# First products with both parts of x as one moving operand of 512 columns, from the fortieth tile on

## The chip, the cores and the metric

The kernel runs on one core of one Trainium2 chip. The core has a matmul engine (TensorE; its weight loads are listed apart as PEld), a vector engine (DVE), a scalar engine (ACT), a general engine (POOL) and a queue engine (SP) that starts transfers. Each takes its own instructions in the order in which the program lists them, and they wait for each other by semaphores. The metric is the time of one execution on the device in microseconds; the number for a kernel is the median of its runs. Before the change it is 1940.97 us, three runs from 1940.72 to 1942.93.

## The reference

Two layers of a decoder trunk on 256 tokens of width 1024. The part that the change touches is the second half of a layer, a retrieval over 16384 experts:

```python
q = (xf @ wq).reshape(T, PEER_HEADS, 2, PEER_KEY_DIM)
s = jnp.einsum('thcd,ckd->thck', q, subkeys).astype(jnp.float32)
sv, si = lax.top_k(s, PEER_TOPK)
...
experts = (ea * PEER_KEYS + eb).reshape(T, PEER_HEADS * PEER_TOPK)
gate = jax.nn.softmax(cv, axis=-1).reshape(T, PEER_HEADS * PEER_TOPK)
...
act = jax.nn.gelu(jnp.einsum('cd,ced->ce', xc, u_tab[ec]))
return jnp.einsum('ce,ced->cd', act * gc, v_tab[ec])
```

Each token takes 128 of the 16384 experts, multiplies itself with their rows of `u_tab`, applies a gelu and a gate, and sums their rows of `v_tab`.

## The kernel before

The kernel gathers nothing. It computes the first product of every token with all 16384 rows of `u_tab`, multiplies by a gate matrix that is zero where a token did not choose an expert, and computes the second product with all of `v_tab`. Both tables are cut into 128 tiles of 128 experts. A tile of `u_tab` is 512 KB: 128 rows of the model's width on the partitions, eight chunks of that width, 128 experts.

**Values in two parts.** The kernel feeds these matmuls in a 32-bit type (`F32R` in the code, fp32r in the trace) to which a value is rounded. So `wtile` (line 96) loads a tile as `raw`, ACT copies it to `hi` (line 103, the rounded value) and DVE, or POOL for the first 14 tiles, subtracts to get `lo`, the rest (line 104). `raw` has four buffers, `hi` and `lo` three each: the pair of a tile takes the place of the pair three tiles before, once TensorE has read that. x is held the same way, in `xThi` and `xTlo`, [128 x 8 chunks x 256 tokens] each, made by `x_split` (line 201). A product is the sum of three: hi with hi, hi with the rest of x, and the rest of the weights with hi (`mm3`, line 110). For a tile of first products `col_mm` (line 114) does this for eight chunks: 24 matmuls of 256 columns, each with its own load of 128 x 128 weights, summed in one half of a PSUM bank of 512 columns.

**First products (`u_tile`, line 739).** Two tiles share a bank. After the odd one ACT applies the gelu to the 512 columns, out of PSUM into a tile `act` of SBUF (line 746), of which there are four, and a transfer from ACT's queue puts it into DRAM (`kept`, line 748).

**What runs beside them.** While a layer's scores are searched for the best 16 (`top`, `pairs`, `choices`, all on DVE), the loop at line 915 puts in tiles of first products by a table of costs. When the choices are known, `turn_round` (line 878) transposes them on TensorE and DVE copies them to `eT` and `gT`. Then 32 groups follow (line 963), each of eight tokens: DVE makes one-hot rows with two operations (`onehots`, lines 939 and 943, called one-hots below), TensorE makes the gate matrix from them with 16 matmuls of 128 columns (line 954), ACT copies it into `G` (line 958). The rest of the first products, but four tiles, stands between these groups, two or three tiles to each. The last four come behind the groups. Then come the second products (`v_tile`, line 1000): 12 matmuls of 512 columns per tile (line 995), with the gated `act` split in two parts as weights.

**Order.** The program is written as straight code; a scheduler sets the order of each engine's instructions from it, and an instruction that waits holds all that stand behind it on its engine. PSUM has eight banks, one pool for all.

Of the kernel before, what the change touches and what calls it, by code (L numbers as in the profile page):

```python
# [12 lines left out]
F32R = mybir.dt.float32r  # L13
# [3 lines left out]
AF = mybir.ActivationFunctionType  # L17
ALU = mybir.AluOpType
# [3 lines left out]
S = 256  # L22
NL = 2
NCH = D // 128
# [23 lines left out]
ROOT_ACT = {1, 2, 3}  # L48
NACT = 4
NPOOL = 14  # L50
NLATE = 4
NCAND = 50
CNT = [16 // (i + 1) for i in range(16)]
# [24 lines left out]
def trunk_kernel(ctx: ExitStack, tc: tile.TileContext, x, xt, cst, lam, pvec, brow, w_in, w_lx, w_v, w_q4, lru_w,  # L78
                 cmp_w1, cmp_w2, w_out, lnrow, wq, sk, u_tab, v_tab, out):
    nc = tc.nc  # L80
    PE, DVE, ACT, POOL = nc.tensor, nc.vector, nc.scalar, nc.gpsimd
    TB = (slice(0, 128), slice(128, 256))
    ALL = slice(0, 256)
    HALF = (slice(0, 256), slice(256, 512))
# [4 lines left out]
    state = ctx.enter_context(tc.tile_pool(name="state", bufs=1))  # L89
    psp = ctx.enter_context(tc.tile_pool(name="psp", bufs=8, space=bass.MemoryType.PSUM))  # L90

    def bank():
        return psp.tile([128, 512], F32, tag="ps", name="ps")


    def wtile(src, shape, lo_eng, dst=None):
        n = int(np.prod(shape))
        raw = ring.tile([128, 1024], F32, tag="raw", name="raw", bufs=4)
        if dst is None:
            dst = (ring.tile([128, 1024], F32R, tag="hi", name="hi"), ring.tile([128, 1024], F32R, tag="lo", name="lo"))  # L100
        nc.sync.dma_start(raw[:, :n], src)
        hi, lo, raw = dst[0][:, :n], dst[1][:, :n], raw[:, :n]
        ACT.copy(hi, raw)  # L103
        lo_eng.tensor_tensor(lo, raw, hi, op=ALU.subtract)  # L104
        if len(shape) == 2:
            hi = hi.rearrange("p (a b) -> p a b", a=shape[0])
            lo = lo.rearrange("p (a b) -> p a b", a=shape[0])
        return hi, lo

    def mm3(ps, a, b, start, stop, order=((0, 0), (0, 1), (1, 0))):  # L110
        for i, (m, n) in enumerate(order):
            PE.matmul(ps, a[m], b[n], start=start and i == 0, stop=stop and i == 2)  # L112

    def col_mm(ps, w, xT, t=ALL):
        for c in range(NCH):
            mm3(ps, (w[0][:, c, :], w[1][:, c, :]), (xT[0][:, c, t], xT[1][:, c, t]), c == 0, c == NCH - 1)

    def row_mm(ps, w, xTf, tb, c, start, stop):
        PE.matmul(ps, xTf[:, c, TB[tb]], w, start=start, stop=stop)  # L119
# [19 lines left out]
            PE.matmul(ps, raw[:, c], xTf[:, c], start=c == 0, stop=c == NCH - 1)  # L139

    def new_xT():
        return (state.tile([128, NCH, S], F32R, name="xThi"), state.tile([128, NCH, S], F32R, name="xTlo"))

    def new_xTf():
        return state.tile([128, NCH, S], F32, tag="xTf", name="xTf")
# [54 lines left out]

    def x_split(xT, s, t):

        ACT.copy(xT[0][:, s, t], xTf[:, s, t])
        DVE.tensor_tensor(xT[1][:, s, t], xTf[:, s, t], xT[0][:, s, t], op=ALU.subtract)

    def ln_gb(new, row):
        gb = [[new(), new()] for _ in range(2)]
# [15 lines left out]
    xT = new_xT()  # L223
    xTf = new_xTf()
    lx = [bank() for _ in range(4)]
    for c0, c1 in ((0, 1), (1, 2), (2, 4), (4, 6), (6, 8)):
        s = slice(c0, c1)
        nc.sync.dma_start(xTf[:, s], xt[:, s])
        w = rtile(w_lx[0, :, s], (c1 - c0, 512))
# [36 lines left out]
    for l in range(NL):  # L266
# [3 lines left out]
        with tc.tile_pool(name="mix", bufs=1, reuse_waits="tile") as mp, \  # L270
# [421 lines left out]
            def nsa_end(qb):  # L692
# [4 lines left out]
                         s=att_scores, w=att_weigh, t=att_trans, v=att_vals, cp=cmp_pv, E=nsa_end,  # L697
# [6 lines left out]
            if l == 0:  # L704
                nc.sync.dma_start(lm, lam)
                psv = [bank(), bank()]
                for c0, c1 in ((0, 3), (3, 6), (6, 8)):
                    w = rtile(w_v[l, :, c0:c1], (c1 - c0, 280))
# [6 lines left out]
            for step in ORDER[l].split():  # L715
                name = step.rstrip("0123456789")
# [3 lines left out]
                elif name == "x":  # L720
                    xT = new_xT()
                    xTf = new_xTf()
# [5 lines left out]
        with tc.tile_pool(name="peer", bufs=1, reuse_waits="tile") as pp:  # L728
# [5 lines left out]
            ub = {}  # L734

            def act_tile():
                return pp.tile([128, 2, S], F32, name="act", bufs=NACT)

            def u_tile(a):
                if a % 2 == 0:  # L740
                    ub[a] = bank()
                ps = ub[a - a % 2]
                col_mm(ps[:, HALF[a % 2]], wtile(u_tab[l, a], (8, 128), POOL if a < NPOOL else DVE), xT)
                if a % 2:
                    at = act_tile()
                    ACT.activation(at.rearrange("p a b -> p (a b)"), ps, AF.Gelu_apprx_tanh)  # L746
                    kept[a - 1] = spill.tile([128, 2, S], F32, name="kept%d" % (a - 1), bufs=1)
                    ACT.dma_start(kept[a - 1], at)

# [530 lines left out]
```

## Time and profile before

| | |
|---|---|
| median of three runs | 1940.97 us (1940.72 to 1942.93) |
| profiled execution | 1938.31 us |
| its span | 1936.5 us |
| TensorE (PE) busy | 1894.0 us, 98% |
| DVE busy | 1330.6 us, 69% |
| ACT busy | 966.3 us, 50% |
| POOL busy | 83.1 us, 4% |
| granted TensorE clock, mean | 0.991 |

The span runs from the first instruction to the last; the execution's own time is 1.8 us longer. All durations come from this one execution, whose time is 2.66 us under the median. Matmuls are pipelined: a matmul's duration in the trace (0.28 us for 256 columns) overlaps the next one's, so the time that a matmul costs in a row of them is the distance between starts. A busy share near 100% therefore says that TensorE had something in flight, and the spacing says how fast it went.

### The profile page before, as it was taken

The page shows a single profiled execution, that of the slowest core. Times are in us where ns is not written, and L with a number is a line of the kernel's source. Part 1 is how long each engine was busy: PE and PEld are TensorE (multiplying, and loading weights), DVE is VectorE, ACT ScalarE, POOL GpSimd, SP SyncE. Part 2 cuts the span into 40 slices and gives each one's busy share as a digit, 9 for nine tenths or more (in the row PEclk, how much of TensorE's full clock was granted, in tenths as well). Part 3 has the DMA queues.
Part 4 walks back from the last instruction along what each step waited for, and adds up shares of the span by engine and source line. Part 5 has one row for each costly group of instructions (what it writes and reads, how often), then busy time and mean ns, then how long its engine had stood idle before and what let it go on. Part 6 is the DMA issues. An engine that isn't in the chain of part 4 may idle for free.

```text
span 1936.5 us, 32461 instructions
## 1 busy us (share of the span) xinstructions
PE 1894.0 (98%) x12580; PEld 1679.2 (87%) x12580; DVE 1330.6 (69%) x2553; ACT 966.3 (50%) x1579; POOL 83.1 (4%) x55
## 2 busy tenths in 40 slices
PE   8999899999999999999999998999999999999998
PEld 7858899999999888888777498999999998888886
DVE  5763994766666776767657549946666656777776
ACT  3635444555555555556445344444555555555553
POOL 0005200000000000000000062000000000000000
PEclk9999999999999999999999999999999999999999
DMA  7505557666667777888362054576666677778783
GB/s 267 175 1 172 153 191 236 211 207 192 204 203 242 244 241 240 282 283 300 140 227 66 0 187 154 189 236 212 196 203 201 201 245 240 244 243 286 250 265 106
DMA packets 130095, 393.91 MB, mean 203 GB/s; under 512 B 15634, under 2 KB 16404, under 8 KB 129812
## 3 DMA queue, kind: packets, MB, share of 16 engines
q1 hardware_dynamic: 111508, 358.28, 57.8%
q10 hardware_dynamic: 18432, 33.56, 4.7%
q8 instruction: 98, 1.61, 0.3%
q14 instruction: 57, 0.47, 0.1%
HBM read 357.18 MB, written 34.60 MB: 202 GB/s over the span
## 4 chain that ended last, share of the span: by engine, by line
PE 88%; DVE 8%; DMA 2%; issue 1%; ACT 1%; SPq 0%; POOL 0%; DVEq 0%; ACTq 0%; POOLq 0%
PE ps L112 39%; PE ps L995 34%; PE ps L954 3%; PE ps L119 3%; PE ps L590 3%; DVE lo L104 1%; PE ps L562 1%; DMA raw<-in_v_tab_dram 1%; PE ps L515 1%; DVE si L789 1%; DVE cd L812 1%; PE ps L232 1%; DVE s L787 1%; DVE si L786 0%; DVE t L866 0%
## 5 line engine op out<-in xcount | busy, mean ns | idle before, releaser
L104 DVE TENSOR_TENSOR lo<-raw,hi 128x1024 fp32r<-128x1024 f32 x516 | 635.1, 1232 | 396.4 <-ACT hi L103 396.0
L103 ACT CAST hi<-raw 128x1024 fp32r<-128x1024 f32 x548 | 575.1, 1050 | 663.4 <-PE ps L112 412.0
L112 PE MATMUL ps<-xThi,lo 128*128 128x256 f32 x2400 | 685.4, 286 | 20.0 <-DVE lo L104 19.7
L112 PE MATMUL ps<-xThi,hi 128*128 128x256 f32 x2400 | 693.5, 289 | 0.0
L112 PE MATMUL ps<-xTlo,hi 128*128 128x256 f32 x2400 | 684.0, 285 | 0.0
L995 PE MATMUL ps<-hi,W 128*128 128x512 f32 x1936 | 517.8, 389 | 0.0
L112 PEld LDWEIGHTS ps<-xThi,lo 128*128 128x128 f32 x2400 | 465.4, 194 | 21.9 <-DVE lo L104 21.2
L112 PEld LDWEIGHTS ps<-xThi,hi 128*128 128x128 f32 x2400 | 465.7, 194 | 0.9 <-issue 0.4
L112 PEld LDWEIGHTS ps<-xTlo,hi 128*128 128x128 f32 x2400 | 465.8, 194 | 0.3
L995 PEld LDWEIGHTS ps<-hi,W 128*128 128x128 f32 x1936 | 363.2, 188 | 75.4
L995 PE MATMUL ps<-lo,W 128*128 128x512 f32 x968 | 298.1, 389 | 0.2 <-DVE lo L104 0.2
L995 PEld LDWEIGHTS ps<-lo,W 128*128 128x128 f32 x968 | 181.6, 188 | 38.2 <-DVE lo L104 0.6
L986 ACT CAST W<-act 128x256 fp32r<-128x256 f32 x242 | 96.1, 402 | 94.6 <-PE ps L995 90.4
L987 DVE TENSOR_TENSOR W<-act,W 128x256 fp32r<-128x256 f32 x242 | 100.0, 422 | 9.5
L104 POOL TENSOR_TENSOR lo<-raw,hi 128x1024 fp32r<-128x1024 f32 x32 | 79.6, 2493 | 355.9 <-ACT hi L103 355.6
L972 DVE TENSOR_TENSOR act<-act,G 128x512 f32<-128x512 f32 x128 | 87.5, 685 | 6.6 <-DMA act<-kept 6.6
L958 ACT ACTIVATE G<-ps 128x256 f32<-128x256 f32 x256 | 81.2, 383 | 5.3
L943 DVE TENSOR_TENSOR ohg<-ohg,gT 128x2048 f16<-128x2048 f16 x64 | 78.2, 1225 | 2.0
L939 DVE TENSOR_TENSOR ohg<-iota,eT 128x2048 f16<-128x2048 f16 x64 | 77.9, 1220 | 0.0
L746 ACT ACTIVATE act<-ps 128x512 f32<-128x512 f32 x128 | 75.7, 591 | 0.1
L954 PE MATMUL ps<-ohg 128*128 128x128 f16 x1024 | 69.9, 219 | 0.0
L954 PEld LDWEIGHTS <-ohg 128*128 128x128 f16 x1024 | 58.8, 97 | 2.8
(256 smaller groups left out, 1179.6 us busy)
## 6 DMA issues: line engine op xcount, KB each, us to landing
raw<-in_u_tab_dram SPq DMA_DIRECT2D x256, 512.0 KB, 3.6
raw<-in_v_tab_dram SPq DMA_DIRECT2D x256, 512.0 KB, 4.2
kept<-act ACTq DMA_DIRECT2D x128, 256.0 KB, 2.5
act<-kept SPq DMA_DIRECT2D x128, 256.0 KB, 4.1
raw<-in_w_in_dram SPq DMA_DIRECT2D x24, 512.0 KB, 4.5
raw<-in_wq_dram SPq DMA_DIRECT2D x24, 512.0 KB, 3.6
ow<-in_w_out_dram SPq DMA_DIRECT2D x16, 512.0 KB, 7.8
qf<-in_w_q_dram SPq DMA_DIRECT2D x8, 512.0 KB, 3.8
```

Source lines behind the costliest of these rows:

```text
L103: ACT.copy(hi, raw)
L104: lo_eng.tensor_tensor(lo, raw, hi, op=ALU.subtract)
L112: PE.matmul(ps, a[m], b[n], start=start and i == 0, stop=stop and i == 2)
L746: ACT.activation(at.rearrange("p a b -> p (a b)"), ps, AF.Gelu_apprx_tanh)
L939: DVE.tensor_tensor(oh.rearrange("p q w a i -> p (q w) a i"), iota.unsqueeze(1).to_broadcast([128, 8, 128, 2]), eT[:, qs].rearrange("p q w ...
L943: DVE.tensor_tensor(og, oh[:, :, 0:1].to_broadcast([128, 4, 2, 128, 2]), gT[:, qs].unsqueeze(3).to_broadcast([128, 4, 2, 128, 2]), op=ALU. ...
L954: PE.matmul(ps[:, k * 128:k * 128 + 128], oh[:, q, 1, :, i], og[:, q, w, :, i], start=w == 0, stop=w == 1)
L958: ACT.activation(G[g][:, :, t1:t1 + 4], ps.rearrange("p (t g a) -> p g a t", g=2, a=64)[:, g], AF.Copy, scale=1.0 / GSC)
L972: i = DVE.tensor_tensor(act[a0], act[a0], G[a0 // 64][:, a0 % 64:a0 % 64 + 2, :], op=ALU.mult)
L986: ACT.copy(whi, at[:, a % 2])
L987: DVE.tensor_tensor(wlo, at[:, a % 2], whi, op=ALU.subtract)
L995: PE.matmul(accs[tb * 2 + hf], ww[m][:, TB[tb]], v[n][:, hf * 512:hf * 512 + 512], start=a == first[0] and (m, n) == (0, 0), stop=a == 127 ...
```

## The change

From the tile `NWIDE` = 40 on, in both layers, a tile of first products is computed by `col_mm2`. Both parts of x now lie in one tile `xT`, [128 x 8 chunks x 2 parts x 256 tokens], so that for one chunk the two parts are 512 columns side by side. One matmul multiplies `hi` with all 512 (the hi part's result goes to the first half of a bank, that of the rest to the second), and one of 256 columns adds `lo` with the hi part to the first half. That makes 16 matmuls per tile. Each tile now takes a bank of its own. Its two halves are added on the way out: ACT copies the second half to `act`, DVE adds the first half to it, and after the odd tile ACT applies the gelu in place, from SBUF to SBUF. Tiles 0 to 39 and all other products run as before, with `xT` in place of `xThi` and `xTlo`.

```diff
--- before.py
+++ after.py
@@ -48,6 +48,7 @@
 ROOT_ACT = {1, 2, 3}
 NACT = 4
 NPOOL = 14
+NWIDE = 40
 NLATE = 4
 NCAND = 50
 CNT = [16 // (i + 1) for i in range(16)]
@@ -111,9 +112,15 @@
         for i, (m, n) in enumerate(order):
             PE.matmul(ps, a[m], b[n], start=start and i == 0, stop=stop and i == 2)
 
-    def col_mm(ps, w, xT, t=ALL):
+    def col_mm(ps, w, xT):
         for c in range(NCH):
-            mm3(ps, (w[0][:, c, :], w[1][:, c, :]), (xT[0][:, c, t], xT[1][:, c, t]), c == 0, c == NCH - 1)
+            mm3(ps, (w[0][:, c], w[1][:, c]), (xT[:, c, 0], xT[:, c, 1]), c == 0, c == NCH - 1)
+
+    def col_mm2(ps, w, xT):
+
+        for c in range(NCH):
+            PE.matmul(ps, w[0][:, c], xT[:, c], start=c == 0, stop=False, skip_group_check=True)
+            PE.matmul(ps[:, :S], w[1][:, c], xT[:, c, 0], start=False, stop=c == NCH - 1, skip_group_check=True)
 
     def row_mm(ps, w, xTf, tb, c, start, stop):
         PE.matmul(ps, xTf[:, c, TB[tb]], w, start=start, stop=stop)
@@ -139,7 +146,7 @@
             PE.matmul(ps, raw[:, c], xTf[:, c], start=c == 0, stop=c == NCH - 1)
 
     def new_xT():
-        return (state.tile([128, NCH, S], F32R, name="xThi"), state.tile([128, NCH, S], F32R, name="xTlo"))
+        return state.tile([128, NCH, 2, S], F32R, name="xT")
 
     def new_xTf():
         return state.tile([128, NCH, S], F32, tag="xTf", name="xTf")
@@ -200,8 +207,8 @@
 
     def x_split(xT, s, t):
 
-        ACT.copy(xT[0][:, s, t], xTf[:, s, t])
-        DVE.tensor_tensor(xT[1][:, s, t], xTf[:, s, t], xT[0][:, s, t], op=ALU.subtract)
+        ACT.copy(xT[:, s, 0, t], xTf[:, s, t])
+        DVE.tensor_tensor(xT[:, s, 1, t], xTf[:, s, t], xT[:, s, 0, t], op=ALU.subtract)
 
     def ln_gb(new, row):
         gb = [[new(), new()] for _ in range(2)]
@@ -738,12 +745,22 @@
 
             def u_tile(a):
                 if a % 2 == 0:
-                    ub[a] = bank()
-                ps = ub[a - a % 2]
-                col_mm(ps[:, HALF[a % 2]], wtile(u_tab[l, a], (8, 128), POOL if a < NPOOL else DVE), xT)
+                    ub[a] = bank() if a < NWIDE else act_tile()
+                w = wtile(u_tab[l, a], (8, 128), POOL if a < NPOOL else DVE)
+                if a < NWIDE:
+                    ps = ub[a - a % 2]
+                    col_mm(ps[:, HALF[a % 2]], w, xT)
+                else:
+                    ps, at = bank(), ub[a - a % 2]
+                    col_mm2(ps, w, xT)
+                    ACT.copy(at[:, a % 2], ps[:, S:])
+                    DVE.tensor_tensor(at[:, a % 2], at[:, a % 2], ps[:, :S], op=ALU.add)
                 if a % 2:
-                    at = act_tile()
-                    ACT.activation(at.rearrange("p a b -> p (a b)"), ps, AF.Gelu_apprx_tanh)
+                    if a < NWIDE:
+                        at = act_tile()
+                        ACT.activation(at.rearrange("p a b -> p (a b)"), ps, AF.Gelu_apprx_tanh)
+                    else:
+                        ACT.activation(at, at, AF.Gelu_apprx_tanh)
                     kept[a - 1] = spill.tile([128, 2, S], F32, name="kept%d" % (a - 1), bufs=1)
                     ACT.dma_start(kept[a - 1], at)
```

In the changed kernel line 105 is the subtraction for `lo`, 122 and 123 are the two matmuls, 756 the copy, 757 the addition, 763 the gelu in place, 903 to 906 `eT` and `gT`, 956 and 960 the one-hots, 971 the gate matmuls.

On TensorE, the end of a group of gate matmuls and the start of the first-product tile behind it, before:

```order
L954 MATMUL ps<-ohg 128x128
L112 MATMUL ps<-xThi,hi 128x256
L112 MATMUL ps<-xTlo,hi 128x256
L112 MATMUL ps<-xThi,lo 128x256
L112 MATMUL ps<-xThi,hi 128x256
```

and with the change:

```order
L971 MATMUL ps<-ohg 128x128
L122 MATMUL ps<-xT,hi 128x512
L123 MATMUL ps<-xT,lo 128x256
L122 MATMUL ps<-xT,hi 128x512
L123 MATMUL ps<-xT,lo 128x256
```

The place of tiles and gates against each other is the same; inside a tile every three rows have become two.

On DVE, the end of the first layer's top-k stretch. Before (the `lo` between the rows of `gT` is that of tile 46, the last row begins with that of tile 47):

```order
L104 TENSOR_TENSOR lo<-raw,hi 128x1024 x16
L886 CAST eT<-ps 128x128x2 x2
L888 TENSOR_SCALAR gT<-ps 128x128x2
L104 TENSOR_TENSOR lo<-raw,hi 128x1024
L889 SCALAR_TENSOR_TENSOR gT<-ps,gT 128x128x2
L939 TENSOR_TENSOR ohg<-iota,eT 128x2048 x2
L943 TENSOR_TENSOR ohg<-ohg,gT 128x2048 x2
L104 TENSOR_TENSOR lo<-raw,hi 128x1024 x6
```

and with the change, from the `lo` of tile 45 to that of tile 47 (the three additions are of tiles 43, 44 and 45):

```order
L105 TENSOR_TENSOR lo<-raw,hi 128x1024
L903 CAST eT<-ps 128x128x2 x2
L757 TENSOR_TENSOR act<-act,ps 128x256
L905 TENSOR_SCALAR gT<-ps 128x128x2
L105 TENSOR_TENSOR lo<-raw,hi 128x1024
L906 SCALAR_TENSOR_TENSOR gT<-ps,gT 128x128x2
L757 TENSOR_TENSOR act<-act,ps 128x256
L956 TENSOR_TENSOR ohg<-iota,eT 128x2048 x2
L960 TENSOR_TENSOR ohg<-ohg,gT 128x2048
L757 TENSOR_TENSOR act<-act,ps 128x256
L960 TENSOR_TENSOR ohg<-ohg,gT 128x2048
L105 TENSOR_TENSOR lo<-raw,hi 128x1024
```

The additions of tiles 43 and 44 now stand before the one-hots, and that of tile 45 among them, ahead of the `lo` of tile 47.

On DVE, in the steady part of the first layer. Before, from the `lo` of tile 93 (the numbers are the program's names of buffers):

```order
L104 TENSOR_TENSOR lo_5551<-raw_5549,hi_5550 128x1024
L104 TENSOR_TENSOR lo_5586<-raw_5584,hi_5585 128x1024
L104 TENSOR_TENSOR lo_5641<-raw_5639,hi_5640 128x1024
L939 TENSOR_TENSOR ohg_5546<-iota_130,eT_1354 128x2048
L943 TENSOR_TENSOR ohg_5546<-ohg_5546,gT_1355 128x2048
L104 TENSOR_TENSOR lo_5676<-raw_5674,hi_5675 128x1024
L104 TENSOR_TENSOR lo_5706<-raw_5704,hi_5705 128x1024
```

and with the change, from the `lo` of tile 93 to that of tile 96 (the additions are of tiles 91 and 92):

```order
L105 TENSOR_TENSOR lo_5348<-raw_5346,hi_5347 128x1024
L105 TENSOR_TENSOR lo_5377<-raw_5375,hi_5376 128x1024
L757 TENSOR_TENSOR act_5216<-act_5216,ps_5273 128x256
L757 TENSOR_TENSOR act_5295<-act_5295,ps_5302 128x256
L956 TENSOR_TENSOR ohg_5343<-iota_129,eT_1352 128x2048
L960 TENSOR_TENSOR ohg_5343<-ohg_5343,gT_1353 128x2048
L105 TENSOR_TENSOR lo_5402<-raw_5400,hi_5401 128x1024
L105 TENSOR_TENSOR lo_5456<-raw_5454,hi_5455 128x1024
```

The `lo` of tile 95 stood before the one-hots and now stands behind them and behind the addition of tile 92.

## Rows read from the trace of the kernel before

**Rows 1.** From the page, busy time of each engine with its share of the span and its instructions.

```profile
PE 1894.0 (98%) x12580; PEld 1679.2 (87%) x12580; DVE 1330.6 (69%) x2553; ACT 966.3 (50%) x1579; POOL 83.1 (4%) x55
```

**Rows 2.** From the page, the chain of work that ended last: shares of the span by engine, then by line.

```profile
PE 88%; DVE 8%; DMA 2%; issue 1%; ACT 1%; SPq 0%; POOL 0%; DVEq 0%; ACTq 0%; POOLq 0%
PE ps L112 39%; PE ps L995 34%; PE ps L954 3%; PE ps L119 3%; PE ps L590 3%; DVE lo L104 1%; PE ps L562 1%; DMA raw<-in_v_tab_dram 1%; PE ps L515 1%; DVE si L789 1%; DVE cd L812 1%; PE ps L232 1%; DVE s L787 1%; DVE si L786 0%; DVE t L866 0%
```

**Rows 3.** From the windows of two stretches of the first layer: length, busy time of each engine with its instructions, the granted clock of TensorE, share and rate of the DMA engines.

```profile
350.00:600.00 250.00, 250.00 (x2329) 248.67 (x2328) 164.15 (x138) 135.48 (x239) 0.00 (x0) 1.00 0.64 204
650.00:900.00 250.00, 250.00 (x1104) 207.01 (x1104) 180.73 (x240) 131.17 (x186) 0.00 (x0) 1.00 0.81 264
```

**Rows 4.** From the waits, all of TensorE's matmuls of line 112: us in total, times, the longest.

```profile
PE ps L112 <- DVE lo L104: 19.7, 8, 4.0
```

**Rows 5.** From the timeline of TensorE, the two matmuls of the first layer's top-k stretch that waited longest: start, us, engine, line, the idle time before and what ended it.

```profile
210.69 0.58 PE L112 MATMUL ps<-xThi,lo 128*128 128x256 f32 x1 [2.73 <-DVE lo L104]
...
261.27 0.39 PE L112 MATMUL ps<-xThi,lo 128*128 128x256 f32 x1 [3.97 <-DVE lo L104]
```

**Rows 6.** From the timeline of TensorE from the end of one first-product tile over a group of gate matmuls into the next tile (its durations overlap: a tile's matmuls are pipelined, and the starts tell the spacing).

```profile
404.37 0.28 PE L112 MATMUL ps<-xThi,lo 128*128 128x256 f32 x1
404.49 1.09 PE L954 MATMUL ps<-ohg 128*128 128x128 f16 x16
405.39 0.36 PE L112 MATMUL ps<-xThi,hi 128*128 128x256 f32 x1
405.59 0.28 PE L112 MATMUL ps<-xTlo,hi 128*128 128x256 f32 x1
...
409.91 0.28 PE L112 MATMUL ps<-xTlo,hi 128*128 128x256 f32 x1
```

**Rows 7.** From the timeline of TensorE in the second products.

```profile
700.36 0.61 PE L995 MATMUL ps<-lo,W 128*128 128x512 f32 x2
700.81 1.07 PE L995 MATMUL ps<-hi,W 128*128 128x512 f32 x4
701.72 0.61 PE L995 MATMUL ps<-lo,W 128*128 128x512 f32 x2
702.17 1.07 PE L995 MATMUL ps<-hi,W 128*128 128x512 f32 x4
703.08 0.61 PE L995 MATMUL ps<-lo,W 128*128 128x512 f32 x2
```

**Rows 8.** From the groups by form of ACT and DVE: operation, out<-in, shapes, count, busy us, mean ns, idle before.

```profile
L103 ACT CAST hi<-raw 128x1024 fp32r<-128x1024 f32 x548 | 575.1, 1050 | 663.4 <-PE ps L112 412.0 <-PE ps L995 181.6 <-issue 12.7
L958 ACT ACTIVATE G<-ps 128x256 f32<-128x256 f32 x256 | 81.2, 383 | 5.3
L746 ACT ACTIVATE act<-ps 128x512 f32<-128x512 f32 x128 | 75.7, 591 | 0.1
L772 ACT COPY qh<-ps 128x256 f32<-128x256 f32 x8 | 2.6, 377 | 0.0
L104 DVE TENSOR_TENSOR lo<-raw,hi 128x1024 fp32r<-128x1024 f32 x516 | 635.1, 1232 | 396.4 <-ACT hi L103 396.0
L476 DVE TENSOR_TENSOR sc<-ps,cmix 128x256 f32<-128x256 f32 x2 | 0.8, 424 | 6.7 <-PE ps L474 6.7
```

**Rows 9.** From the timeline of ACT, two casts of `hi`, that of tile 46 and one in the steady part.

```profile
340.45 1.05 ACT L103 CAST hi<-raw 128x1024 fp32r<-128x1024 f32 x1 [1.83 <-PE ps L112]
...
404.57 1.05 ACT L103 CAST hi<-raw 128x1024 fp32r<-128x1024 f32 x1 [1.83 <-PE ps L112]
```

**Rows 10.** From the timeline of DVE at the end of the top-k stretch, around the first one-hots.

```profile
340.80 0.76 DVE L886 CAST eT<-ps 128x256 f16<-128x256 f32 x2 [0.92 <-PE ps L883]
341.47 0.42 DVE L888 TENSOR_SCALAR gT<-ps 128x256 f16<-128x256 f32 x1
341.80 1.22 DVE L104 TENSOR_TENSOR lo<-raw,hi 128x1024 fp32r<-128x1024 f32 x1
342.93 0.42 DVE L889 SCALAR_TENSOR_TENSOR gT<-ps,gT 128x256 f16<-128x256 f32 x1
343.26 2.35 DVE L939 TENSOR_TENSOR ohg<-iota,eT 128x2048 f16<-128x2048 f16 x2
345.53 2.36 DVE L943 TENSOR_TENSOR ohg<-ohg,gT 128x2048 f16<-128x2048 f16 x2
347.80 2.36 DVE L104 TENSOR_TENSOR lo<-raw,hi 128x1024 fp32r<-128x1024 f32 x2
```

**Rows 11.** From the timeline of TensorE at the same place: the transposes of `turn_round` behind tile 43, the second matmul of tile 44, and the first of tile 47.

```profile
340.38 0.60 PE L883 MATMUL ps<-cst_sb,ev 128*128 128x128 f32 x4
341.15 0.28 PE L112 MATMUL ps<-xTlo,hi 128*128 128x256 f32 x1
...
349.67 0.28 PE L112 MATMUL ps<-xThi,hi 128*128 128x256 f32 x1
```

**Rows 12.** From the windows ahead of and behind the matmul at 210.69 us, columns as in rows 3.

```profile
207.40:210.70 3.30, 0.57 (x6) 0.37 (x5) 3.30 (x24) 0.00 (x0) 0.00 (x0) 0.97 0.00 0
210.70:214.00 3.30, 3.30 (x15) 3.30 (x16) 3.27 (x9) 2.60 (x4) 0.00 (x0) 0.51 0.54 159
```

## The prediction

> **What bounds the kernel now.** I read the busy shares and the chain of waits first [rows 1, 2]: TensorE is busy for 98% of the span and holds 88% of the chain, with 39% of the span on line 112, the first products (`u_tile`), and 34% on line 995, the second products. Then the windows of two stretches [rows 3]: while first products and gate matrices are made (350 to 600 us) and while second products run (650 to 900 us) TensorE is busy for all 250 us at clock 1.00, DVE for 164 and 181 us, ACT for 135 and 131 us. The waits [rows 4] give line 112 only 19.7 us of idle time in eight waits, and the two long ones of the first layer (2.73 us at 210.69, 3.97 us at 261.27 [rows 5]) lie in the top-k stretch, before tile 40 is reached. So around the change the bound is how fast TensorE takes its matmuls. Two things count: the time of a tile on TensorE, and whether `lo` and `hi` of the next tiles still come in time.
>
> **One tile on TensorE.** In a first-product tile the matmuls of 256 columns start 0.12 us apart: 405.59 to 409.91 us is 4.32 us for 36 of them, none at a wider step [rows 6]. The second products of 512 columns take 1.36 us for six (700.36, 701.72, 703.08), 0.2267 us each, a new weight load before each one [rows 7]. The two spacings differ by 0.1067 us for 256 columns, 2.4 columns per ns, the higher of the clock's two levels (2.4 GHz). At that rate 256 columns take 0.1067 and 512 take 0.2133 us, so in both cases 0.0133 us per matmul is left that does not depend on its columns. A tile now: 24 x 0.12 = 2.88 us. After: 8 x (0.2267 + 0.12) = 2.773 us. The columns are the same 6144; eight matmuls go, with eight fixed parts: 0.107 us. Wide tiles: 88 per layer (40 to 127), 176 in all, 18.8 us. Nothing else on TensorE's path changes: its order is that of before with each tile's 24 matmuls as 16, and 1408 matmuls and weight loads are gone.
>
> Bounds. No row has a 512-column matmul of these 32-bit values followed by one of 256. Were the 256-column one, its weights loaded under a longer stream, charged only what the gate matmuls are (0.90 us for sixteen of 128 columns is 0.056 us, 0.003 us over their columns [rows 6]), the gain would be 8 x 0.0103 us more per tile, 14.5 us in all. The second products speak against it: their weights load under 512 columns and they still pay 0.0133 us [rows 7]. At the other end, a 512-column matmul costing two of 256 (0.24 us) would gain nothing. I take 0.2267 us, measured on the same kind of operand.
>
> The Trainium skill, "TensorE: Matmul & The Clock Gate", section "Back-to-back issue gap", speaks against the change: it gives columns divided by 2.4 plus 2.5 ns per matmul at full clock. By it a tile would go from 2.62 to 2.60 us and the change would be worth 3.5 us. The gate matmuls agree (56 ns against its 55.8); the first and second products do not, 120 and 227 ns against 109 and 216, and on these the measurement decides.
>
> **What is added on the way out.** Per tile ACT copies 256 columns out of PSUM and DVE adds the other half of the bank. Both operations have rows: 0.377 us (line 772) and 0.424 us (line 476, one input in PSUM) [rows 8]. That is 66 us more on ACT and 75 us more on DVE. The gelu moves from a PSUM input to an SBUF one; I leave it at 0.59 us. In a cycle of seven tiles and three groups of gates TensorE takes 7 x 2.773 + 3 x 0.98 = 22.4 us (0.98 us: gates at 404.49, regular spacing back at 405.47 [rows 6]); DVE has 7 x (1.23 + 0.42) + 3 x 2.46 = 18.9 us, ACT 7 x (1.05 + 0.38) + 12 x 0.38 + 3.5 x 0.59 = 16.6 us. Neither becomes the bound by its sum. Both finish one instruction before the next, though, and the new ones wait for the end of a tile: what stands behind them waits too, above all `lo` (DVE) and `hi` (ACT).
>
> In the steady part the dearest place is a = 95 (in one such place in twelve tiles two additions stand close before the one-hots; six per layer). Count from the end of tile 92, with 0.08 us from a tile's end to ACT, as from 404.49 to 404.57 [rows 6, 9]. The one-hots ahead end at -2.43 (the addition of 90, up to -4.89, stood before them), `lo` of 93 and 94 follow to 0.03, the addition of 91 at 0.45, the gelu runs 0.53 to 1.12, the copy of 92 to 1.50, its addition 1.58 to 2.00, the two one-hot operations to 4.46, `lo` of 95 to 5.69. TensorE meanwhile makes the gates (0.98) and tiles 93 and 94, and wants this `lo` after the first matmul of tile 95, at 6.76. Margin 1.07 us: hidden. At the other tiles it is larger. Cost taken: nothing; if the cover went, up to about 1.5 us at each of 12 places.
>
> The one place where the cover does not reach is a = 47, behind the first one-hots. Before: `lo` of 47 and 48 run from 347.80 us, the first done near 349.0, and tile 47 starts at 349.67 [rows 10, 11], so it came in time by 0.9 us. Now count from 340.38, the end of tile 43. Tile 44 follows the transposes at 0.65 (341.15 less one step of 0.12 [rows 11]), and tile 46 ends at 0.65 + 3 x 2.773 = 8.97. On ACT `hi` of 46 runs 0.1 to 1.15 as before [rows 9], then the copy of 43 to 1.5. On DVE the addition of 43 goes to 1.95, `gT`, `lo` of 46 and `gT` to 3.75 (their steps in [rows 10]), the addition of 44 to 4.35 (its copy waits for tile 44, 3.42), two one-hots and one product to 7.7 at 1.13 each (343.26 to 345.53 is two), the addition of 45 to 8.2, the second product to 9.3, and only then `lo` of 47 to 10.5. It is wanted at 8.97 + 0.23. TensorE waits 1.3 us, once per layer: 2.6 us. Bounds: 0, if the copies come earlier than I count, and about 3 us per layer if the wait pulls the clock down: after the 2.73 us wait at 210.69 the granted clock was 0.51 for 3.3 us [rows 12], which costs 1.65 us. I take 1.3, as this wait is half as long as those that show it.
>
> The rest costs nothing. The last tile's copy and addition stand before the second products, whose first `lo` and weights are made one tile earlier. One tile `xT` in place of two, and its split, keep their order and waits. A bank per tile instead of per two: eight banks turn in about four tiles. The DMA queue has the same transfers; a u tile's `raw` comes four tiles ahead.
>
> **Sum.** -18.8 + 2.6 = -16.2 us. The profiled execution took 1938.31 us (span 1936.5), so 1922.1 there; it lies 2.66 us under the median of 1940.97, on which the forecast stands: 1924.8 us. A measurement of this kernel tells about 0.2% from no change, 3.9 us.
>
> **Rivals.**
> 1. The margins at the 12 dear places are gone, because copy and addition take longer beside TensorE's writes to the other banks than in the rows. Each 0.25 us more on both takes 1.07 us of margin and makes waits of 1.1 to 1.7 us. 12 x 1.5 = 18 us would eat the gain: 1942.8 at worst, 1930 to 1940 likely. For: ACT's `hi` already starts only when a tile ends [rows 9]. Against: both durations come from the same operations with PSUM inputs.
> 2. Slower: DVE's queue decides at every group of one-hots. Additions hold `lo` back as at a = 47, in place of the 6.8 us of cover only one tile. 62 groups x 1.3 us = 81 us less 18.8: 2003. From 23 us of waits in all, 0.37 us per group, it is slower than before by what can be measured. Against: after a = 47 every `lo` stands two tiles ahead, and margins over 1 us would have to vanish everywhere.
> 3. Of the 0.0133 us only what the gate matmuls show, 0.003 us, goes with a matmul, the rest with its columns: 8 x 0.003 x 176 = 4.2 us gained. -4.2 + 2.6: 1939.4, no change. The rule of the Trainium skill named above ("TensorE: Matmul & The Clock Gate", "Back-to-back issue gap") comes to the same within a microsecond. Against: the second products [rows 7].
> 4. The 256-column matmuls become cheaper behind long ones: 14.5 us more, 1910.
>
> **How the numbers follow.** Forecast 0.70, with its own range 1920 to 1930 (no wait at a = 47 to one of 3 us with a few small ones); rival 1 0.13, rival 2 0.07, rival 3 0.06, rival 4 0.04. The range to 1935 takes in the better half of rival 1, and 1919 a little of rival 4: 0.80. Faster by over 0.2% (under 1937.1): 0.70 + 0.04 + most of rival 1, 0.84. Within 0.2%: rival 3 and a little of rival 1, 0.08. Slower: rival 2 and 0.01, 0.08.
>
> **What would show it.** Starts in a wide tile 0.227 and 0.12 us apart in turn, 2.77 us per tile; copy near 0.38 and addition near 0.42 us; one wait of line 123 for `lo` near 340 us and its twin in the second layer, 1 to 1.5 us each; TensorE without idle time from there to the second products. Waits for `lo` at a = 59, 71, 83, 95, 107 or 119 would be rival 1, waits behind each pair of one-hots rival 2, a spacing of 0.24 us or 0.11 us rivals 3 and 4. The forecast is wrong if the tile's time is not 2.77 us or the waits exceed 6 us.

## The result and the profile after

The changed kernel takes 1928.72 us, the median of four runs from 1928.28 to 1929.19, against 1941.22 us for the kernel before (four runs, 1940.72 to 1942.93; the fourth has moved the median from 1940.97): ratio 0.9937, 95% interval 0.9921 to 0.9952. The forecast was 1924.8 us with 1919 to 1935 as its range. The profiled execution took 1928.28 us (span 1926.5), 10.0 us less than that of before, the medians 12.5 less.

From the page, busy time and the chain by line; beside them [rows 1, 2]:

```profile
PE 1879.1 (98%) x11169; PEld 1595.0 (83%) x11172; DVE 1388.4 (72%) x2729; ACT 1021.4 (53%) x1755; POOL 82.9 (4%) x55
...
PE ps L1012 34%; PE ps L122 16%; PE ps L113 13%; PE ps L123 8%; PE ps L971 3%; PE ps L126 3%; PE ps L597 3%; DVE lo L105 2%; DMA raw<-in_v_tab_dram 1%; PE ps L239 1%; PE ps L569 1%; PE ps L522 1%; DVE si L806 1%; DVE cd L829 1%; DVE s L804 1%
```

TensorE has 1411 matmul records fewer (1408 are left out by the change) and is still 98% busy. First products now stand on three lines, 16, 13 and 8% of the chain, 37% for 39.

From the windows, the same two stretches as in [rows 3]:

```profile
350.00:600.00 250.00, 250.00 (x1762) 218.20 (x1761) 192.67 (x219) 163.39 (x325) 0.00 (x0) 1.00 0.67 211
650.00:900.00 250.00, 250.00 (x1105) 207.01 (x1104) 182.30 (x241) 132.89 (x187) 0.00 (x0) 1.00 0.81 266
```

Among the first products DVE went from 164 to 193 us of 250 and ACT from 135 to 163; TensorE has no gap and keeps the full clock. The second products read as before.

From the waits of all the kernel, TensorE's of the first products; beside them [rows 4]:

```profile
PE ps L113 <- DVE lo L105: 20.8, 9, 4.0
...
PE ps L123 <- DVE lo L105: 1.9, 2, 0.9
```

The wide tiles wait twice for `lo`, 0.93 us each. The narrow ones wait as they did. From the groups, the subtraction, the addition, the copy and the gelu in place, beside [rows 8]:

```profile
L105 DVE TENSOR_TENSOR lo<-raw,hi 128x1024 fp32r<-128x1024 f32 x516 | 634.5, 1231 | 291.1 <-ACT hi L104 287.8
...
L757 DVE TENSOR_TENSOR act<-act,ps 128x256 f32<-128x256 f32 x176 | 73.3, 416 | 42.2 <-ACT act L756 41.8
...
L756 ACT COPY act<-ps 128x256 f32<-128x256 f32 x176 | 64.1, 364 | 27.0 <-PE ps L123 24.7 <-DMA raw<-in_u_tab_dram 2.2
L763 ACT ACTIVATE act<-act 128x512 f32<-128x512 f32 x88 | 55.7, 633 | 66.2 <-DVE act L757 66.2
```

Now the spacing. From the timeline of TensorE, the end of one group of tiles, the gates, and the start of the next group:

```profile
399.60 0.40 PE L122 MATMUL ps<-xT,hi 128*128 128x512 f32 x1
399.83 0.28 PE L123 MATMUL ps<-xT,lo 128*128 128x256 f32 x1
399.95 0.39 PE L122 MATMUL ps<-xT,hi 128*128 128x512 f32 x1
...
400.99 0.40 PE L122 MATMUL ps<-xT,hi 128*128 128x512 f32 x1
...
402.67 0.40 PE L122 MATMUL ps<-xT,hi 128*128 128x512 f32 x1
402.91 0.28 PE L123 MATMUL ps<-xT,lo 128*128 128x256 f32 x1
403.02 0.40 PE L122 MATMUL ps<-xT,hi 128*128 128x512 f32 x1
403.25 0.28 PE L123 MATMUL ps<-xT,lo 128*128 128x256 f32 x1
403.37 0.40 PE L122 MATMUL ps<-xT,hi 128*128 128x512 f32 x1
403.61 0.28 PE L123 MATMUL ps<-xT,lo 128*128 128x256 f32 x1
403.73 0.40 PE L122 MATMUL ps<-xT,hi 128*128 128x512 f32 x1
...
405.14 0.40 PE L122 MATMUL ps<-xT,hi 128*128 128x512 f32 x1
```

Ahead of the gates four pairs take 1.39 us (399.60 to 400.99), 0.347 each, as forecast. Behind them seven take 2.47 us (402.67 to 405.14), 0.353. From the first gates on, every group of tiles keeps one of these two spacings, 0.3467 or 0.3533 us a pair, from its start to its end, and behind the next gates it is the other one. Ahead of the first gates, tiles 40 to 43 run at 0.3533, tiles 44 to 46 at 0.3467, and 47 to 49, behind the wait for `lo`, at 0.3533. A tile is thus 2.773 or 2.827 us, 2.80 in the mean.

Two lengths tell what that comes to. From the timeline of TensorE before, the first matmul behind a group of gates, that behind the fifth group after it, and the first second product:

```profile
359.21 0.36 PE L112 MATMUL ps<-xThi,hi 128*128 128x256 f32 x1
...
398.65 0.36 PE L112 MATMUL ps<-xThi,hi 128*128 128x256 f32 x1
...
614.20 0.63 PE L995 MATMUL ps<-hi,W 128*128 128x512 f32 x2
```

and with the change, from the transposes of `turn_round` (before they start at 340.38 [rows 11]):

```profile
337.63 0.60 PE L900 MATMUL ps<-cst_sb,ev 128*128 128x128 f32 x4
...
357.17 0.48 PE L122 MATMUL ps<-xT,hi 128*128 128x512 f32 x1
...
395.70 0.47 PE L122 MATMUL ps<-xT,hi 128*128 128x512 f32 x1
...
606.15 0.62 PE L1012 MATMUL ps<-hi,W 128*128 128x512 f32 x2
```

Twelve tiles with five groups of gates took 39.44 us before and take 38.53 now: 0.076 us less per tile, where 0.107 was forecast. From the transposes to the first second product it is 273.82 us before and 268.52 after, in both layers alike, so 10.6 us in all; tiles 40 to 43, ahead of that stretch, add 4 x 0.053 = 0.2 us per layer. That makes 11.0 us. Outside, the two traces differ in ways that no run ties to the change: the changed kernel comes to the first transposes 2.7 us earlier (0.2 of it by the tiles just named), and from the first layer's second products to the second layer's transposes it takes 3.0 us longer; in twelve of the thirteen traces of this case (all but run 1's) these two lengths scatter from 337.5 to 340.7 and from 688 to 695 us. Most of those 3.0 us lie in the second layer's mixing stage, where TensorE waits 3.9 us at line 377 (3.2 before) and then runs at a granted clock of 0.54 for 4.7 us (1.00 before).

### The profile page after: what moved, and what is told of

It is laid out like the page before. It is cut to its first block, busy times and chain, and to the rows that moved or that the text cites. A ratio compares the mean times of both kernels' runs of the same rounds, so it can differ in the third digit from the quotient of the medians.

```text
span 1926.5 us, 30094 instructions
## 1 busy us (share of the span) xinstructions
PE 1879.1 (98%) x11169; PEld 1595.0 (83%) x11172; DVE 1388.4 (72%) x2729; ACT 1021.4 (53%) x1755; POOL 82.9 (4%) x55
## 4 chain that ended last, share of the span: by engine, by line
PE 87%; DVE 9%; DMA 2%; issue 1%; ACT 1%; POOL 0%; SPq 0%; DVEq 0%; ACTq 0%; POOLq 0%
PE ps L1012 34%; PE ps L122 16%; PE ps L113 13%; PE ps L123 8%; PE ps L971 3%; PE ps L126 3%; PE ps L597 3%; DVE lo L105 2%; DMA raw<-in_v_tab_dram 1%; PE ps L239 1%; PE ps L569 1%; PE ps L522 1%; DVE si L806 1%; DVE cd L829 1%; DVE s L804 1%
## 5 line engine op out<-in xcount | busy, mean ns | idle before, releaser
L122 PE MATMUL ps<-xT,hi 128*128 128x512 f32 x1408 | 501.2, 400 | 0.0
L123 PE MATMUL ps<-xT,lo 128*128 128x256 f32 x1408 | 392.8, 279 | 1.9 <-DVE lo L105 1.9
L113 PE MATMUL ps<-xT,hi 128*128 128x256 f32 x1984 | 369.2, 288 | 0.0
L113 PEld LDWEIGHTS ps<-xT,hi 128*128 128x128 f32 x1984 | 315.5, 195 | 1.2 <-issue 0.4
L122 PEld LDWEIGHTS ps<-xT,hi 128*128 128x128 f32 x1408 | 264.2, 188 | 60.0
L113 PE MATMUL ps<-xT,lo 128*128 128x256 f32 x992 | 285.2, 288 | 21.4 <-DVE lo L105 20.8
L123 PEld LDWEIGHTS ps<-xT,lo 128*128 128x128 f32 x1408 | 265.3, 188 | 2.8 <-DVE lo L105 2.7
L113 PEld LDWEIGHTS ps<-xT,lo 128*128 128x128 f32 x992 | 193.4, 195 | 23.6 <-DVE lo L105 22.6
L1004 DVE TENSOR_TENSOR W<-act,W 128x256 fp32r<-128x256 f32 x242 | 100.6, 422 | 11.2 <-ACT W L1003 0.9
L757 DVE TENSOR_TENSOR act<-act,ps 128x256 f32<-128x256 f32 x176 | 73.3, 416 | 42.2 <-ACT act L756 41.8
L763 ACT ACTIVATE act<-act 128x512 f32<-128x512 f32 x88 | 55.7, 633 | 66.2 <-DVE act L757 66.2
```

The source lines that it names most:

```text
L122: PE.matmul(ps, w[0][:, c], xT[:, c], start=c == 0, stop=False, skip_group_check=True)
L123: PE.matmul(ps[:, :S], w[1][:, c], xT[:, c, 0], start=False, stop=c == NCH - 1, skip_group_check=True)
L757: DVE.tensor_tensor(at[:, a % 2], at[:, a % 2], ps[:, :S], op=ALU.add)
L1004: DVE.tensor_tensor(wlo, at[:, a % 2], whi, op=ALU.subtract)
```

## The experiments

Two theories at first. A: the additional 0.0067 us per pair belongs to long and short matmuls in turn. B: it comes from the new traffic of ACT's copy and DVE's addition beside them. The first four kernels ran on one chip (kernel before: 1937.64 us, 17 runs), the next four on a second (1939.01, 9 runs), the last three on a third (1938.52, 9 runs); ratios are to the kernel before on the same chip. The intervals of most runs overlap with that of the changed kernel, so the times seldom decide between theories; the spacings in the traces do, and the stretch, which repeats within 0.02 us from layer to layer. "The stretch" is from the transposes to the first second product, in one layer.

**1. Long ones first.** The eight matmuls of 512 columns of a tile, then its eight of 256:

```diff
         for c in range(NCH):
             PE.matmul(ps, w[0][:, c], xT[:, c], start=c == 0, stop=False, skip_group_check=True)
+        for c in range(NCH):
             PE.matmul(ps[:, :S], w[1][:, c], xT[:, c, 0], start=False, stop=c == NCH - 1, skip_group_check=True)
```

> Inside a wide tile all eight matmuls of 512 columns come first, then the eight of 256; the same products. Theory A (the extra 0.0067 us that a pair costs in every second group of tiles comes from the alternation of 512 and 256 columns, by the phase in which a group starts behind the gates): starts 0.2267 us apart, then 0.12, in every group, 2.773 us per tile; no wait for lo behind the first one-hots, since lo is wanted 1.6 us later; 18.8 us under the kernel before, about 1922.5. Theory B (the extra comes from ACT's copy and DVE's addition, which read the banks and write SBUF beside the matmuls): every second group still takes about 0.05 us more per tile; only the two waits of 0.93 us go, about 1927.

Ratio 0.9944 (0.9930 to 0.9958), which on this chip is about 1927 us, B's number; it left no trace from which a spacing can be read, so it was run again as 6.

**2. No copy, no addition.** The gelu reads the first half of the bank alone:

```diff
-                    ACT.copy(at[:, a % 2], ps[:, S:])
-                    DVE.tensor_tensor(at[:, a % 2], at[:, a % 2], ps[:, :S], op=ALU.add)
+                    ACT.activation(at[:, a % 2], ps[:, :S], AF.Gelu_apprx_tanh)
...
-                    else:
-                        ACT.activation(at, at, AF.Gelu_apprx_tanh)
```

> Wide tiles as in the changed kernel, but without the copy and the addition: the gelu takes the first half of each bank alone, 256 columns per tile. It leaves out the product of hi with the rest of x for tiles 40 to 127. Theory A: pairs of 0.3467 and 0.3533 us alternate group by group as before, no wait behind the first one-hots, about 18.8 - 4.8 = 14 us under the kernel before: 1927. Theory B: all pairs at 0.3467 us, 18.8 us under it: 1922.5.

1925.19 us, ratio 0.9943 (0.9925 to 0.9961). Both spacings are there, group by group, in the same places, and twelve tiles with five groups of gates take 38.53 us as in the changed kernel. B falls. The wait at tile 47 is gone, and the stretch is 267.18 us. Behind the first gates every group takes as long as in the changed kernel, so the 268.52 - 267.18 = 1.34 us are what the wait costs there.

**3. Copy and addition, but matmuls of one width.** The 512 columns as two matmuls of 256 into the two halves of the bank (its sums are off by 2.8%, for a reason that was not looked into; instructions and bytes are those of 24 matmuls):

```diff
-            PE.matmul(ps, w[0][:, c], xT[:, c], start=c == 0, stop=False, skip_group_check=True)
+            PE.matmul(ps[:, :S], w[0][:, c], xT[:, c, 0], start=c == 0, stop=False, skip_group_check=True)
+            PE.matmul(ps[:, S:], w[0][:, c], xT[:, c, 1], start=c == 0, stop=False, skip_group_check=True)
```

> The way out alone: 24 matmuls of 256 columns per tile as in the kernel before, but hi with the rest of x goes to the second half of the tile's own bank, and copy and addition as in the changed kernel. Same results. Theory A: 0.12 us per matmul everywhere, one wait for lo of 1 to 1.5 us per layer, about 2 us over the kernel before: 1943. Theory B: the spacing rises above 0.12 us in some groups, 5 us and more: 1946 or over.

1937.54 us, ratio 1.0000 (0.9991 to 1.0009), the stretch 273.81 and 273.83 us for 273.82 before. Every group has one spacing, 0.12 us, from its timeline:

```profile
406.13 0.28 PE L122 MATMUL ps<-xT,hi 128*128 128x256 f32 x1
406.25 0.28 PE L123 MATMUL ps<-xT,hi 128*128 128x256 f32 x1
406.37 0.28 PE L124 MATMUL ps<-xT,lo 128*128 128x256 f32 x1
406.49 0.28 PE L122 MATMUL ps<-xT,hi 128*128 128x256 f32 x1
```

So 176 copies, 176 additions, the one tile for x and a bank per tile cost nothing while TensorE takes 2.88 us per tile. All that the change gains is on TensorE. The wait for `lo` that was expected did not come: at that place the scheduler has set another order on DVE, with the `lo` of tile 47 ahead of the addition of tile 45 and of the second one-hot product. So this run says nothing of that wait.

**4. The order long, short, short, long.**

```diff
-            PE.matmul(ps, w[0][:, c], xT[:, c], start=c == 0, stop=False, skip_group_check=True)
-            PE.matmul(ps[:, :S], w[1][:, c], xT[:, c, 0], start=False, stop=c == NCH - 1, skip_group_check=True)
+            for i in ((0, 1) if c % 2 == 0 else (1, 0)):
+                if i == 0:
+                    PE.matmul(ps, w[0][:, c], xT[:, c], start=c == 0, stop=c == NCH - 1, skip_group_check=True)
+                else:
+                    PE.matmul(ps[:, :S], w[1][:, c], xT[:, c, 0], start=False, stop=False, skip_group_check=True)
```

> The order inside a wide tile is 512, 256, 256, 512, 512, 256, 256, 512 and so on: half as many steps from a short to a long matmul. Theory A: the extra of the slow groups is halved or goes, 2.4 us or more less: 1924 to 1926. Theory B: no difference from the changed kernel, 1928.7.

1925.26 us, ratio 0.9937 (0.9920 to 0.9954). Eleven double pairs from 402.50 to 410.17 us take 7.67 us, 0.3486 a pair, and every group has this value: the two speeds are gone, for one between them. Twelve tiles with five groups take 38.42 us; the stretch is 266.96 us, with 0.04 us of idle time left at tile 47. The time is the one of theory A, but the ratio is that of the changed kernel on its chip, so only the spacing speaks for A. From its timeline:

```profile
402.50 0.40 PE L126 MATMUL ps<-xT,lo 128*128 128x256 f32 x2
402.73 0.63 PE L124 MATMUL ps<-xT,hi 128*128 128x512 f32 x2
403.20 0.39 PE L126 MATMUL ps<-xT,lo 128*128 128x256 f32 x2
...
410.17 0.39 PE L126 MATMUL ps<-xT,lo 128*128 128x256 f32 x2
```

**5 and 6. The changed kernel again, and long ones first again**, on one chip.

> The changed kernel again, as it is, so that the others have it beside them on the same chip. Both theories: ratio to the kernel before 0.993 to 0.994, and again two spacings of a pair of 512 and 256 columns, 0.3467 and 0.3533 us, that change from one group of tiles to the next behind every group of gates.

> Eight matmuls of 512 columns, then eight of 256, in each wide tile, once more. Theory A (the 0.0067 us comes where the width changes): the width changes once a tile and not every matmul, so a tile takes 8 x (0.2267 + 0.12) = 2.77 us in nearly every group, and the time is some 4 us below the changed kernel of the same chip. Theory B (it comes from traffic of the copies and additions): the pattern of two speeds by groups stays, and so does the time.

The changed kernel: 1930.33 us, 0.9948 (0.9931 to 0.9965), the same spacings in the same places, the stretch again 268.52. Long first: 1925.44 us, 0.9925 (0.9908 to 0.9943). A's 2.773 us per tile was not met, though: from its timeline,

```profile
404.46 2.00 PE L122 MATMUL ps<-xT,hi 128*128 128x512 f32 x8
406.30 1.12 PE L124 MATMUL ps<-xT,lo 128*128 128x256 f32 x8
407.25 2.00 PE L122 MATMUL ps<-xT,hi 128*128 128x512 f32 x8
```

a tile takes 2.79 us in all groups, eight long matmuls 1.84 (8 x 0.2267 = 1.81) and eight short 0.95. Twelve tiles with five groups take 38.47 us, hardly less than 38.53. B's two speeds by groups are gone as well, so neither expectation was met. Its stretch is 266.96 us, 1.56 less than the changed kernel's, mainly because tile 47's `lo` is now wanted eight long matmuls later and the wait is gone.

**7 and 8. What sets the speed of a group.** A1: a phase that the gates hand on; A2: the buffer of the one-hots, of which there are two in turn, one in `state` (tag `xTf`), one in the pool.

Run 7 exchanges the two:

```diff
-                    ohg = (state.tile([128, 2, 4, 2, 128, 2], F16, tag="xTf", name="ohg") if t0 % 16 else
+                    ohg = (state.tile([128, 2, 4, 2, 128, 2], F16, tag="xTf", name="ohg") if t0 % 16 == 0 else
```

Run 8 puts one more matmul ahead of a group's sixteen:

```diff
+                        if h == 0:
+                            PE.matmul(ps[:, 0:128], oh[:, 0, 1, :, 0], og[:, 0, 0, :, 0], start=True, stop=True)
```

> The two buffers of the one-hots change places (the first, third, ... group of gates reads the one in state, the others the one in the pool). Theory A1 (the speed of a group is set by the phase in which it starts behind the gates): fast and slow groups stay where they are, the time is that of the changed kernel within 1 us. Theory A2 (it is set by the buffer of one-hots that is written or read beside the group): fast and slow groups change places, and the time stays within 1 us.

> One more matmul of 128 columns ahead of every group of gates (17 for 16; its product is overwritten), 64 in all by 0.056 us = 3.6 us. Theory A1 (phase): the groups no longer take turns as before, all of one speed: all fast gives 4.8 us back, so about 1 us below the changed kernel; all slow costs 4.8 us more, so about 8 us above it. Theory A2 (buffer): fast and slow still take turns, and it is 3.6 us above the changed kernel.

Run 7: 1929.42 us, 0.9950 (0.9932 to 0.9969), order of all instructions unchanged, and the fast and the slow groups change places, all of them (stretch 268.63 us). From its timeline, a group that took 0.3533 us a pair in the changed kernel:

```profile
403.00 0.40 PE L122 MATMUL ps<-xT,hi 128*128 128x512 f32 x1
...
404.39 0.40 PE L122 MATMUL ps<-xT,hi 128*128 128x512 f32 x1
```

Four pairs take 1.39 us. Run 8: 1932.67 us, 0.9964 (0.9952 to 0.9977); both speeds occur, but no longer in turn: two groups at 0.3467 us, one at 0.3533, three at 0.3467, then six at 0.3533. The stretch is 2.17 us longer, 1.79 of it for 32 more gate matmuls. So neither theory holds alone: the buffer matters, and so does the number of matmuls between the groups.

**9 and 10. One buffer for all one-hots.** Made behind the first tile of a group, when the gates before have read it:

```diff
                 for i in range(32):
-                    following = onehots(8 * i + 8) if i < 31 else None
                     while a < 128 - NLATE and (a - a0) * 32 < (i + 1) * (128 - NLATE - a0):
                         u_tile(a)
                         a += 1
+                        if made is None:
+                            made = onehots(8 * i)
                     gates(8 * i, *made)
-                    made = following
+                    made = None
```

In run 9 `ohg` is always the tile of `state`, in run 10 always that of the pool.

> All groups of gates read their one-hots from one buffer, the one in state; they are made behind the first tile of the group, since the buffer is free only behind the gates before. Theory A2 (the buffer that the gates read sets the speed of the group behind them): every group of tiles at 0.3467 us a pair, twelve tiles and five groups of gates in 38.3 us for 38.53 in the changed kernel, as long as PE does not wait for the one-hots. Theory A1 (a phase that the gates hand on): the two speeds still both occur.

> The same with the one buffer in the pool. Theory A2: every group at 0.3533 us a pair, twelve tiles and five groups of gates in 38.85 us, some 3 us a layer more than with the buffer in state. Theory A1: both speeds occur, and the two kernels differ by less than 1 us.

Run 9: 1925.82 us, 0.9934 (0.9918 to 0.9949). Run 10: 1929.41 us, 0.9955 (0.9939 to 0.9970). The instructions of the two come in the same order on every engine; the one difference is the place of the one-hots in memory. With the pool's buffer every group is slow, twelve tiles with five groups take 38.84 us and the stretch 269.34; from its timeline:

```profile
403.39 0.40 PE L122 MATMUL ps<-xT,hi 128*128 128x512 f32 x1
403.63 0.28 PE L123 MATMUL ps<-xT,lo 128*128 128x256 f32 x1
403.75 0.40 PE L122 MATMUL ps<-xT,hi 128*128 128x512 f32 x1
403.99 0.28 PE L123 MATMUL ps<-xT,lo 128*128 128x256 f32 x1
404.11 0.40 PE L122 MATMUL ps<-xT,hi 128*128 128x512 f32 x1
```

With that of `state` the speeds still take turns, 38.54 us, stretch 267.33. So A2 came true in run 10 and failed in run 9. The changed kernel and runs 7, 9 and 10 fit one rule: gates that read the pool's buffer leave the next group slow; gates that read `state`'s leave it at the other speed than before. Run 8 does not fit it, and the rule names no cause. In neither run does a wide tile wait for `lo`. Half the groups slow for all slow is 269.34 - 267.33 = 2.0 us per layer. Half of them slow for none is as much: 38 of the 78 tiles behind the first gates are slow, at 0.053 us each.

**11. Wide tiles from the 24th on**, long ones first: `NWIDE = 24` in the kernel of 6.

> Wide tiles from the 24th on, with the eight long matmuls first: 16 more wide tiles a layer in the stage where the top-k work is on DVE. If PE bounds that stage too: 2 x 16 x 0.08 = 2.6 us below the kernel with long matmuls first from the 40th on (ratio 0.991). If the sixteen additions, 0.42 us each, make lo late there: no gain, or up to 2 x 16 x 0.42 = 13 us more.

1922.69 us (1921.98 to 1925.13), 0.9925 (0.9912 to 0.9939), the lowest time of all. By the medians it is 15.8 us under the kernel before on its chip, where 6 had 13.6; by the ratios, 0.9925 both, they are the same. The times cannot tell 6 and 11 apart. The traces can: in the first layer, where both have the same waits, the time from the start of the last row of first-product tiles beside the top-k work (250.32 us in 6, 250.93 in 11) to the transposes is 87.9 us in 6 and 86.5 in 11: 1.4 us for sixteen tiles. From the waits of 11, 160 to 620 us,

```profile
PE ps L113 <- DVE lo L105: 8.3, 3, 4.3
```

and none by a wide tile; run 6 has this same row. Sixteen additions in the top-k stage made nothing late there.

## Why the prediction was right or wrong

**What bounds the kernel.** Right. From tile 40 on TensorE has no idle time among the first products but the one wait per layer, and run 3 shows that without fewer matmuls nothing is gained or lost.

**One tile on TensorE: -18.8 us.** Right in kind, but this is the term that was mis-sized, and by the prediction's own sign (a tile's time that is not 2.77 us) the step is wrong. It is the one that ends in "I take 0.2267 us, measured on the same kind of operand": a spacing from a row of equal matmuls, taken for a row of unequal ones. It holds in every other group, and in the rest a pair costs 0.0067 us more. For the stretch's 84 tiles (44 to 127) 84 x 0.107 = 9.0 us per layer were due; 273.82 - 267.18 = 6.6 came where no wide tile waits (run 2). Of the 2.3 lost, 2.0 are the slow groups (runs 9 and 10). The rest stands at the start of the groups: two tiles behind gates take 5.637 us in a fast group and 5.735 in a slow one, 0.09 and 0.08 over their sixteen pairs, where 48 equal matmuls take 5.837, 0.077 over theirs. That is 0.01 us for each of 32 groups, 0.3 us. Tiles 40 to 43, all slow, lose another 0.2. In both layers that is about 5 us. Run 2 shows that copies and additions are not the cause, runs 3 and 4 that it belongs to the order of unequal matmuls, runs 7 to 10 that the buffer that the gates read has a part in which groups are slow. Why a mixed row runs at two speeds stays open.

**What is added on the way out: nothing.** Right, shown by run 3 behind the first one-hots. The copy took 0.364 us and the addition 0.416 for the 0.377 and 0.424 forecast. The gelu from SBUF took 0.633 us, not 0.59; it is hidden, ACT being 65% busy. At a = 59, 71, 83, 95, 107 and 119 no wait appeared.

**One wait at a = 47: 1.3 us per layer.** Right in place and price. From the timeline of TensorE:

```profile
346.84 0.39 PE L122 MATMUL ps<-xT,hi 128*128 128x512 f32 x1
348.15 0.39 PE L123 MATMUL ps<-xT,lo 128*128 128x256 f32 x1 [0.93 <-DVE lo L105]
348.37 0.40 PE L122 MATMUL ps<-xT,hi 128*128 128x512 f32 x1
```

and of DVE just ahead of it:

```profile
344.28 1.22 DVE L960 TENSOR_TENSOR ohg<-ohg,gT 128x2048 f16<-128x2048 f16 x1
345.41 0.41 DVE L757 TENSOR_TENSOR act<-act,ps 128x256 f32<-128x256 f32 x1
345.74 1.22 DVE L960 TENSOR_TENSOR ohg<-ohg,gT 128x2048 f16<-128x2048 f16 x1
346.88 1.22 DVE L105 TENSOR_TENSOR lo<-raw,hi 128x1024 fp32r<-128x1024 f32 x1
```

The addition of tile 45 stands between the two products of the one-hots as counted, and `lo` of 47 runs from 346.88, 1.22 us long. 0.93 us of idle time are shown, and 1.34 us are what the stretch gains without it (run 2): 1.1 on tile 47, 0.2 on the next two, which run at the slow spacing behind the wait. The granted clock stayed at 1.00. The place hangs on the order that the scheduler sets: in run 3, with another order, the wait is not there.

**Sum.** -18.8 + 2 x 2.5 + 2 x 1.3 = -11.2 us, where the traces show 11.0 from tile 40 on; the medians differ by 12.5, and the ratio's interval is 9.3 to 15.3 us.

**Rivals.** 1 and 2 fell: no place but a = 47 waits. 3 fell: a pair would take 0.36 us by it, and the gain is three times what it allows. Its sign, 0.24 us behind a long matmul, is there all the same, at every third one of a slow group (403.37 to 403.61). The rule of the Trainium skill ("TensorE: Matmul & The Clock Gate", section "Back-to-back issue gap") would have given 3.5 us, an estimate by its 2.5 ns per matmul; the trace disagrees, with 13 ns per matmul in a fast group (0.3467 us for 768 columns at 2.4 GHz, 0.32 us). The section gives the 2.5 ns for an isolated matmul; for a row in which each has its own weight load, as here, it states about 81 ns at 128 columns and 131 at 512, and the 56 and 227 ns of [rows 6, 7] disagree with these as well. 4 fell: no group takes less than 0.3467 us a pair.

## What to carry to other kernels

Where TensorE is full, putting two products with the same weights side by side as one moving operand saves a fixed part per matmul: 0.013 us by rows of one width, 0.010 as measured here (6.6 us for 84 x 8 matmuls). Adding the halves on the way out was free here, where the queues of ACT and DVE had room. Price a mixed order of long and short matmuls from rows of that very mix. Long ones first gave one speed, 2.79 us a tile, and let the second operand come later, by up to 1.6 us per tile (1.84 us of long matmuls ahead of the first short one, for 0.23). Where additions join a queue, look for the place where a helper stands right behind a burst: here that was where a wait appeared.

## What was not expected of the hardware

The same instructions in the same order run at two speeds, 0.3467 and 0.3533 us for a matmul of 512 and one of 256 columns with their weight loads, and the speed stays for a whole group of 32 or 48 matmuls. 0.0067 us is 16 cycles of the 2.4 GHz clock. It is no even stretching: in a fast group long matmuls start 0.35 and 0.34 us apart in turn, in a slow one 0.35, 0.35 and 0.36 (402.67, 403.02, 403.37, 403.73), so one pair in three is dearer. Why, no run shows. Moving the one buffer that the 16 matmuls ahead of the group read changes the speed (run 7, and run 9 against 10), and one more such matmul too (run 8); a wait inside a group can as well (fast ahead of the wait at tile 47, slow behind it). Rows of equal matmuls show nothing of it (run 3). Which property of the buffer does it, its address or something set by it, stays open; moving the pool's buffer alone was not tried.
